# Row sums of squared differences: the first load pair recorded with the others instead of ahead of SyncE's drain

## The chip, the core and the metric

The kernel runs on one core of a Trainium2 chip. The time is device microseconds of one execution, here the median of three. Beside it stands a profile of one execution, taken by the hardware profiler. The engines of the core are TensorE (PE), VectorE (DVE), ScalarE (ACT), GpSimd (POOL) and SyncE (SP). SyncE computes nothing; its queue issues every DMA of this kernel. TensorE has no work in it.

## The reference

Two arrays of 1024 x 4096 float32 are subtracted, squared and summed along each row:

```python
def reference(x, y, axis):          # axis = -1
    return np.sum((x - y) ** 2, axis=axis).astype(np.float32)
```

So 33.55 MB are read from HBM and 4 KB are written.

## The kernel before

**Tiling.** Each of the 128 partitions takes 8 neighbouring rows (`R = B // P`, line 61), so a partition's share of `x` is one stretch of 8 x 4096 numbers in HBM. The tensors `X` and `Y` in SBUF hold 6 rows a partition (`H`, line 69). Rows 6 and 7 are loaded into the places of rows 0 and 1 once these are done with; column numbers are taken modulo 6 rows (lines 93 and 111).

**Loads.** `load_pair` (line 98) issues one DMA for a stretch of columns of `x` and one for the same stretch of `y`, both on SyncE, with a semaphore of their own. The first pair brings rows 0 to 3 (16,384 numbers a partition, 8.4 MB each for `x` and `y`), the second rows 4 and 5. Row 6 comes in two chunks (`w6`, line 75) and row 7 in six (`w7`, line 76). These eight pairs are issued behind a wait for ScalarE's second square (line 156), since they write over rows 0 and 1.

**Work on a row or chunk.** VectorE waits for the pair's landing, subtracts `Y` from `X` in place (`sub`, line 113), and then ScalarE squares and sums (line 121), or, for three of the chunks (`squares`, line 77), VectorE does so itself (line 129). `add_up` (line 144) adds the sums of chunks. The last chunk's square starts from the sum of the others, which stands in `head`. Then SyncE stores the 8 results of each partition (line 189) and waits for the store to land.

**What sets the order.** The kernel uses no scheduler; it records its instructions and puts them into the program's entry block itself, with the class `Program`. This block is made by the launch code (line 208 in the profile) and holds, engine by engine, a first part in which GpSimd sets four constants and all engines meet: each engine drains and raises a semaphore, GpSimd waits for all of them, raises a second semaphore, and each engine passes on that one. After this meeting the block ends in a branch for each engine. `Program._take` (line 24) takes what has been recorded since the last time; `_put` (line 29) inserts it at a given place in the entry block. There are two callers:

- `early` (line 32) inserts ahead of the drain of one engine, so what it moves runs on that engine ahead of the meeting;
- `close` (line 42), called once at the end, inserts all the rest ahead of the first branch, behind the meeting.

In the kernel before, `early` is called once, with SyncE, when only the first load pair has been recorded (lines 105 to 107):

```python
    load_pair(0, 4 * D)
    prog.early(mybir.EngineType.SP)
    load_pair(4 * D, 6 * D)
```

So SyncE issues the pair of rows 0 to 3 as its first instructions, then drains and meets the other engines, and then issues the pair of rows 4 and 5. All other work of the kernel stands behind the meeting on each engine. The two places and the two helpers that the diff does not touch but that decide where instructions land are in the code below.

Of the kernel before, what the change touches and what calls it, by code (L numbers as in the profile page):

```python
# [1 line left out]
_os.environ.setdefault("NEURON_RT_ULTRASERVER_MODE", "4")  # L2

# [3 lines left out]


class Program:

    def __init__(self, nc, tc):
        self.nc, self.hook = nc, tc.instruction_hook
        self.here = nc.cur_bb.bb.instructions
        self.entry = nc.main_func.blocks[0].instructions
        nc.remove_inst_callback(self.hook)  # L20
        self.lower, nc._always_lower_symbolic_ap = nc._always_lower_symbolic_ap, False
        self.before = len(self.here)

    def _take(self):
        taken = self.here[self.before :]
        del self.here[self.before :]
        return taken

    def _put(self, where):
        self.entry[where:where] = self._take()  # L30

    def early(self, engine):

        self._put(
            next(
                n
                for n, i in enumerate(self.entry)
                if i.engine == engine and str(i.opcode) == "Drain"
            )
        )  # L40

    def close(self):

        self._put(
            next(
                n for n, i in enumerate(self.entry) if str(i.opcode) == "UnconditionalBranch"
            )
        )
        self.nc._always_lower_symbolic_ap = self.lower
        self.nc.push_inst_callback(self.hook)  # L50


def kernel(tc, x, y, axis, out):
    nc = tc.nc
    P = nc.NUM_PARTITIONS
    F32 = mybir.dt.float32
    Square = mybir.ActivationFunctionType.Square
    mult, add = mybir.AluOpType.mult, mybir.AluOpType.add

    B, D = x.shape  # L60
    R = B // P


    xv = x.rearrange("(p r) d -> p (r d)", p=P)
    yv = y.rearrange("(p r) d -> p (r d)", p=P)
    ov = out.rearrange("(p r) -> p r", p=P)


    H = 6
    X = nc.alloc_sbuf_tensor("X", [P, H * D], F32).ap()  # L70
    Y = nc.alloc_sbuf_tensor("Y", [P, H * D], F32).ap()
    results = nc.alloc_sbuf_tensor("results", [P, R], F32).ap()
    junk = nc.alloc_psum_tensor("junk", [P, D], F32).ap()

    w6 = [3328, 768]
    w7 = [1280, 1024, 640, 512, 320, 320]
    squares = "ADAAAADD"
    assert sum(w6) == sum(w7) == D
    K = len(w7)
    part6 = nc.alloc_sbuf_tensor("part6", [P, len(w6)], F32).ap()  # L80
    part7 = nc.alloc_sbuf_tensor("part7", [P, K - 1], F32).ap()
    head = nc.alloc_sbuf_tensor("head", [P, 1], F32).ap()

    diffs = tc.alloc_semaphore("diffs")
    acts = tc.alloc_semaphore("acts")
    sums = tc.alloc_semaphore("sums")
    stored = tc.alloc_semaphore("stored")
    n = dict(diffs=0, acts=0, sums=0)

    prog = Program(nc, tc)  # L90

    def load(sem, src, dst, c0, c1):
        h0 = c0 % (H * D)
        nc.sync.dma_start(out=dst[:, h0 : h0 + c1 - c0], in_=src[:, c0:c1]).then_inc(sem, 16)  # L94

    loaded = []

    def load_pair(c0, c1):
        sem = tc.alloc_semaphore("loaded%d" % len(loaded))
        load(sem, xv, X, c0, c1)  # L100
        load(sem, yv, Y, c0, c1)
        loaded.append(sem)


    load_pair(0, 4 * D)
    prog.early(mybir.EngineType.SP)
    load_pair(4 * D, 6 * D)


    def sub(c0, w):  # L110
        h0 = c0 % (H * D)
        a = X[:, h0 : h0 + w]
        nc.vector.tensor_sub(out=a, in0=a, in1=Y[:, h0 : h0 + w]).then_inc(diffs, 1)  # L113
        n["diffs"] += 1

    def square_on_act(c0, w, acc):
        h0 = c0 % (H * D)
        nc.scalar.wait_ge(diffs, n["diffs"])
        if n["acts"]:
            nc.scalar.wait_ge(acts, n["acts"])  # L120
        nc.scalar.activation(  # L121
            out=junk[:, 0:w], in_=X[:, h0 : h0 + w], func=Square, accum_out=acc
        ).then_inc(acts, 1)
        n["acts"] += 1

    def square_on_dve(c0, w, acc, start):
        h0 = c0 % (H * D)
        nc.vector.wait_ge(diffs, n["diffs"])
        nc.vector.tensor_tensor_reduce(  # L129
            out=Y[:, h0 : h0 + w],  # L130
            in0=X[:, h0 : h0 + w],
            in1=X[:, h0 : h0 + w],
            scale=1.0,
            scalar=start,
            op0=mult,
            op1=add,
            accum_out=acc,
        ).then_inc(sums, 1)
        n["sums"] += 1

    def add_up(acc, parts, after=None):
        nc.vector.wait_ge(acts, n["acts"] if after is None else after)
        nc.vector.wait_ge(sums, n["sums"])  # L143
        nc.vector.tensor_reduce(  # L144
            out=acc, in_=parts, axis=mybir.AxisListType.X, op=add
        ).then_inc(sums, 1)
        n["sums"] += 1

    for r in range(6):
        if r in (0, 4):  # L150
            nc.vector.wait_ge(loaded[r // 4], 32)
        sub(r * D, D)
        square_on_act(r * D, D, results[:, r : r + 1])
        if r == 1:

            nc.sync.wait_ge(acts, 2)
            c0 = 6 * D
            for w in w6 + w7:
                load_pair(c0, c0 + w)
                c0 += w  # L160

    c0 = 6 * D
    for k, w in enumerate(w6 + w7):
        k7 = k - len(w6)
        if k7 == K - 1:
            add_up(head, part7)
        nc.vector.wait_ge(loaded[2 + k], 32)
        if k7 == K - 1:
            nc.vector.wait_ge(sums, n["sums"])  # L169
        sub(c0, w)  # L170
        if k7 < 0:
            acc = part6[:, k : k + 1]
        elif k7 < K - 1:
            acc = part7[:, k7 : k7 + 1]
        if k7 == K - 1:
            square_on_dve(c0, w, results[:, 7:8], head)
        elif squares[k] == "A":
            square_on_act(c0, w, acc)
        else:
            square_on_dve(c0, w, acc, 0.0)  # L180
        if k7 == 2:
            add_up(results[:, 6:7], part6, after=acts6)
        if k7 == -1:
            acts6 = n["acts"]
        c0 += w

    nc.sync.wait_ge(sums, n["sums"])
    nc.sync.wait_ge(acts, n["acts"])
    nc.sync.dma_start(out=ov, in_=results).then_inc(stored, 16)
    nc.sync.wait_ge(stored, 16)  # L190
    prog.close()


# [1 line left out]
_INS = ['x', 'y', 'axis']  # L195
_OUTS = [((1024,), 'float32')]

_NUMBERS = {'axis': -1}


# [26 lines left out]
```

## Time and profile before

| what | value |
|---|---|
| time, median of 3 runs | 86.94 us (86.9, 86.94, 87.03) |
| time of the profiled execution | 87.03 us |
| span of the profiled execution, first to last instruction | 85.2 us |
| bytes loaded, mean rate over the span | 33.56 MB, 394 GB/s |
| VectorE busy | 38.0 us (45%) |
| ScalarE busy | 30.7 us (36%) |
| first issue of a load to its landing (`x`, rows 0 to 3) | 21.9 us |
| issue of its `y` half to its landing | 40.8 us |
| first subtraction starts | 41.24 us |
| last sum ends, store issued | 82.88 us, 82.91 us |

Times in the profile count from the first instruction of the span. In lists of instructions the engine's name with a q (SPq, POOLq) stands for its sequencer: waits, drains and DMA issues, in which the engine itself is not busy. `L94` is line 94 of the kernel; all loads have that line, since `load` issues them. `L208` is the launch code with its meeting, `L222` the end of the program, where the engines meet again. `X<-in_x_dram` is a DMA or instruction that writes `X` from the array named. In the chain of waits each step is followed back to what released it; the shares there are of the span. A DMA share of 1.00 means that all 16 DMA engines of the core moved data all the time.

### The profile page before, as it was taken

How to read it: one execution, taken by the hardware profiler on the slowest of the kernel's cores; microseconds unless marked ns; L12 is line 12 of the kernel's file. 1: busy time of each engine (PE TensorE's matmuls, PEld its weight loads, DVE VectorE, ACT ScalarE, POOL GpSimd, SP SyncE). 2: the span in 40 equal slices, each digit the busy share in tenths (PEclk: the TensorE clock that was granted, in tenths of full speed). 3: DMA queues.
4: the chain of work that ended last, by engine and by line, in shares of the span. 5: the costliest groups of instructions: out<-in, count | busy, mean ns of one | idle time of the engine just before them, and what ended most of it. 6: DMA issues, size and time to landing. Idle time of an engine off the chain costs nothing.

```text
span 85.2 us, 122 instructions
## 1 busy us (share of the span) xinstructions
DVE 38.0 (45%) x22; ACT 30.7 (36%) x23; POOL 0.2 (0%) x4
## 2 busy tenths in 40 slices
DVE  0000000000000000000699999995599999997670
ACT  4100000000000000000005979797924979999800
POOL 0000000000000000000000000000000000000000
DMA  9559999997499999993899979997999999999700
GB/s 492 246 246 492 492 492 492 492 492 338 215 431 492 492 492 492 492 461 154 369 492 477 415 338 492 492 400 338 412 412 437 372 426 423 408 401 383 262 0 2
DMA packets 3024, 33.56 MB, mean 394 GB/s; under 512 B 464, under 2 KB 976, under 8 KB 2256
## 3 DMA queue, kind: packets, MB, share of 16 engines
q1 hardware_dynamic: 3024, 33.56, 93.8%
HBM read 33.55 MB, written 0.00 MB: 394 GB/s over the span
## 4 chain that ended last, share of the span: by engine, by line
DMA 63%; SPq 15%; DVE 13%; ACT 4%; issue 1%; DVEq 0%
DMA Y<-in_y_dram 63%; SPq L94 15%; DVE X L113 11%; ACT junk L121 4%; DVE Y L129 1%; DVE head L144 0%; DVEq L169 0%; DVEq L143 0%; DVE part L129 0%; DVEq L222 0%
## 5 line engine op out<-in xcount | busy, mean ns | idle before, releaser
L113 DVE TENSOR_TENSOR X<-X,Y 128x4096 f32<-128x4096 f32 (+7 forms) x14 | 35.8, 2594 | 44.7 <-DMA Y<-in_y_dram 44.6
L121 ACT ACTIVATE junk<-X 128x4096 f32<-128x4096 f32 (+5 forms) x11 | 28.1, 2550 | 49.0 <-DVE X L113 48.6
L121 ACT ACTIVATION_READ_ACCUMULATOR junk<-X 128x1 f32 x11 | 2.0, 186 | 0.0
L121 ACT ACT_TABLE_LOAD x1 | 1.3, 1283 | 1.3 <-PEq L208 1.3
L129 DVE CUSTOM_DVE_ANT_0 Y<-X 128x768 f32<-128x768 f32 (+1 forms) x2 | 1.4, 724 | 0.1
L129 DVE CUSTOM_DVE_ANT_0 Y<-X,head 128x320 f32<-128x320 f32 x1 | 0.6, 552 | 0.0
L144 DVE TENSOR_REDUCE head<-part 128x1 f32<-128x5 f32 x1 | 0.2, 158 | 0.1
L129 DVE DVE_READ_ACCUMULATOR2_ANT part<- 128x1 f32 x2 | 0.2, 82 | 0.0
L144 DVE TENSOR_REDUCE results<-part 128x1 f32<-128x2 f32 x1 | 0.1, 150 | 0.0
L208 POOL MEMSET const-bfloat16-1.0<- 128x1 bf16 x1 | 0.1, 101 | 0.0
L208 POOL MEMSET const-uint8-127<- 128x1 uint8 x1 | 0.1, 101 | 0.0
L208 POOL MEMSET const-float32-0.0<- 128x1 f32 x1 | 0.1, 98 | 0.2 <-issue 0.2
L208 POOL MEMSET const-float32-1.0<- 128x1 f32 x1 | 0.1, 98 | 0.0
L129 DVE DVE_READ_ACCUMULATOR2_ANT results<- 128x1 f32 x1 | 0.1, 83 | 0.0
## 6 DMA issues: line engine op xcount, KB each, us to landing
X<-in_x_dram SPq DMA_DIRECT2D x1, 4096.0 KB, 49.7
Y<-in_y_dram SPq DMA_DIRECT2D x1, 4096.0 KB, 59.0
X<-in_x_dram SPq DMA_DIRECT2D x1, 1664.0 KB, 10.9
Y<-in_y_dram SPq DMA_DIRECT2D x1, 1664.0 KB, 14.6
X<-in_x_dram SPq DMA_DIRECT2D x1, 640.0 KB, 16.7
Y<-in_y_dram SPq DMA_DIRECT2D x1, 640.0 KB, 17.8
X<-in_x_dram SPq DMA_DIRECT2D x1, 512.0 KB, 18.6
Y<-in_y_dram SPq DMA_DIRECT2D x1, 512.0 KB, 19.4
```

The costliest lines, as they stand in the source:

```text
L94: nc.sync.dma_start(out=dst[:, h0 : h0 + c1 - c0], in_=src[:, c0:c1]).then_inc(sem, 16)
L113: nc.vector.tensor_sub(out=a, in0=a, in1=Y[:, h0 : h0 + w]).then_inc(diffs, 1)
L121: nc.scalar.activation(out=junk[:, 0:w], in_=X[:, h0 : h0 + w], func=Square, accum_out=acc).then_inc(acts, 1)
L129: nc.vector.tensor_tensor_reduce(out=Y[:, h0 : h0 + w], in0=X[:, h0 : h0 + w], in1=X[:, h0 : h0 + w], scale=1.0, scalar=start, op0=mult, o ...
L144: nc.vector.tensor_reduce(out=acc, in_=parts, axis=mybir.AxisListType.X, op=add).then_inc(sums, 1)
L208: nc = _bacc.Bacc("TRN2", target_bir_lowering=False, num_devices=1)
```

## The change

The call of `early` is deleted. The first pair is then taken by `close` with all the rest, and stands behind the meeting of the entry block, ahead of the second pair. `early` itself stays, and nothing calls it. The whole diff:

```diff
     load_pair(0, 4 * D)
-    prog.early(mybir.EngineType.SP)
     load_pair(4 * D, 6 * D)
```

The order of each engine's instructions is otherwise the same; on SyncE the changed program has the drain and the wait of the meeting first, then the X and Y loads of rows 0 to 3, then those of rows 4 and 5, then the wait for ScalarE and the chunks of rows 6 and 7. All line numbers behind 106 are lower by one.

## The prediction, made before the result was known

> **What bounds the kernel now.** I read the chain of waits first, to see which work ended last, then the DMA slices and windows, to see whether that work has slack anywhere, then the opening of the timeline and the group of instructions of line 208, because that is where the change acts.
>
> The head of the chain of work that ended last, from the page:
>
> ```profile
> ## 4 chain that ended last, share of the span: by engine, by line
> DMA 63%; SPq 15%; DVE 13%; ACT 4%; issue 1%; DVEq 0%
> ```
>
> The same chain in order of time, cut to its roots and its end (start us, us, what):
>
> ```profile
> 0.43 40.79 DMA Y<-in_y_dram
> ...
> 50.04 3.72 ACT junk L121 x2
> ...
> 67.14 13.24 DMA Y<-in_y_dram
> 80.38 0.02 issue
> 80.40 0.51 DVE X L113
> ```
>
> The chain starts at the very first load pair: the Y half of rows 0 to 3 is issued at 0.43 us and lands 40.79 us later. Everything after hangs on it, because VectorE's first subtraction waits for that landing, ScalarE's second square (done at 53.76) lets SyncE issue rows 6 and 7, and the last transfer of the chain ends at 80.38. From there to the last sum at 82.9 VectorE works almost without a break.
>
> Does the load stream ever pause, so that a late start could be made up? The DMA view and a table of windows (us, then busy time of the engines, clock, DMA share, GB/s):
>
> ```profile
> q1 hardware_dynamic: 3024, 33.56, 93.8%
> ...
> 0.00:20.00 20.00, 0.00 (x0) 1.28 (x1) 0.20 (x4) 1.00 1.00 419
> 20.00:40.00 20.00, 0.00 (x0) 0.00 (x0) 0.00 (x0) 1.00 0.97 419
> 40.00:60.00 20.00, 17.43 (x4) 12.42 (x7) 0.00 (x0) 1.00 0.99 426
> 60.00:80.00 20.00, 18.18 (x11) 16.25 (x14) 0.00 (x0) 1.00 1.01 406
> ```
>
> The share of the 16 DMA engines that is busy is 0.97 to 1.01 in all four quarters (a packet is booked in the window where it starts, hence values over 1). The trace's packet records say the same more sharply: between the first load packet at 1.00 us and the stream's tail near 80 us there is no moment without packets in flight, and 16 of them are in flight on average. So the kernel is one unbroken transfer of 33.55 MB, with a start of about 1.0 us ahead of it and a tail of VectorE and the store behind it.
>
> The start, from the timeline (start us, us, instruction):
>
> ```profile
> 0.00 0.38 SPq L94 DMA_DIRECT2D X<-in_x_dram  x1
> ...
> 0.33 0.10 POOL L208 MEMSET const-uint8-127<- 128x1 uint8 x1
> 0.43 0.42 SPq L94 DMA_DIRECT2D Y<-in_y_dram  x1
> 1.25 1.28 ACT L121 ACT_TABLE_LOAD   x1 [1.25 <-PEq L208]
> 1.26 0.33 SPq L94 DMA_DIRECT2D X<-in_x_dram  x1
> ```
>
> SyncE issues the first pair as its first two instructions. Line 208, the launch code, then has all engines meet: each drains, tells GpSimd through a semaphore, and GpSimd releases them. SyncE's second pair stands behind that release, at 1.26. The group of line 208 (duration in ns, then first and last start):
>
> ```profile
> L208 POOLq DRAIN  x1: 179/179/179, 0.3 to 0.3; - x1
> ...
> L208 SPq DRAIN  x1: 125/125/125, 0.9 to 0.9; - x1
> L208 SPq EVENT_SEMAPHORE  x1: 17/17/17, 1.2 to 1.2; - x1
> ```
>
> **The change, part by part.** It deletes the one call that puts what has been recorded so far ahead of SyncE's drain. The built order of the changed kernel shows the result: the first pair now stands where the second stood, directly behind the release of the meeting, and the second pair follows it. No instruction is added or removed on any engine, and only SyncE's order differs.
>
> *What it removes.* Two issues (0.38 and 0.42 us, with a gap of 0.05) ahead of SyncE's drain. In the trace's own records the drain runs from 0.905 to 1.030 us. All other engines have arrived earlier: VectorE and ScalarE drain at 0.12 and 0.13, TensorE at 0.31, GpSimd ends its drain at 0.479, behind its four memsets. So SyncE is the last one at the meeting today, and it holds the meeting by 1.030 - 0.479 = 0.55 us.
>
> *What the release costs.* From SyncE's drain end at 1.030 GpSimd sees all arrivals at 1.056, sends the release at 1.134, SyncE passes at 1.176, and the next issue starts at 1.259: 0.229 us in all.
>
> *The new start.* SyncE drains at once. The last arrival is then GpSimd at 0.479, whose instructions I take to stay where they are. Adding 0.229 gives 0.708. One link differs, since GpSimd now waits for its own arrival and not for SyncE's: at the meeting at the kernel's end, where GpSimd too is late, its drain ends at 85.022 and it sees the arrivals at 85.066, 0.044 after, in place of 0.026. That gives 0.726. I take 0.72. The X issue moves from 0.00 to 0.72, and the Y issue behind it from 0.43 to about 1.15.
>
> *Bounds.* From below: if GpSimd were in time as well and only the release remained, the issue would stand at 0.007 (a drain with nothing ahead of it, as SyncE's drains at the end have) + 0.229 = 0.24. From above: if the release did not move at all, because something other than SyncE's arrival sets it, the issue would stand at today's 1.26. The value lies at 0.72 by the nearest row, GpSimd's drain.
>
> The Trainium skill, page "Runtime: NRT & Kernel Launch", section "The ~15µs preamble/postamble breakdown", puts a crossing of the five engines on the runtime's own sync barrier at some 355 ns, at 44 ns a hop. By that figure the start would be 0.479 + 0.355 + 0.083 (from passing to issue) = 0.92, an estimate, and the time 87.86; the row of this trace has 0.15 for that crossing, and the sum goes by the row.
>
> *What it moves.* The first load packet starts 1.00 us after the X issue today; the same distance gives 1.72. As the stream has no pause, its end moves by the same 0.72, and with it every landing. No later step is late on its own account: the second pair's issue moves from 1.26 to about 1.6, but its packets come up only after 16.8 MB of the first pair, near 41 us, so this is covered by 39 us. The issues of rows 6 and 7 start at 53.77, behind ScalarE's second square, which moves with the Y landing; the queue ahead of them still holds the second pair until 60.67, so they keep 6.9 us of cover. SyncE's long issues (up to 3.44 us, behind a full queue) move along with the queue. VectorE waits for landings up to 80.40 (idle 0.20, 0.43, 0.47 and 0.23 us ahead of its last four subtractions that waited, each ended by a Y transfer), so it cannot swallow a late landing.
>
> *What gets earlier.* The release comes 0.55 us earlier for the other engines. ScalarE's table load moves from 1.25 to about 0.7, but ScalarE has nothing to do until 45.70, and VectorE until the first landing. This gain is worth nothing.
>
> The Trainium skill's page "DMA: Bandwidth & Descriptors", section "Issuing engines are not separate DMA queues", calls the sequencer's time to start a DMA usually small beside the DMA itself. Read as a rule about this change it speaks for no difference (86.94): 0.38 us of issuing against 21.9 us of transfer. The issue is not lengthened here, though, it starts later, and a stream without a pause cannot hide a late start.
>
> **Sum.** The profiled execution took 87.03 us, with a span of 85.2, so 1.8 us lie around the span, which I leave as they are. 87.03 + 0.72 = 87.75 for that execution; it is the slowest of the three shown, 0.09 over their median. On the median: 86.94 + 0.72 = **87.66 us**. One small unknown goes the other way: should the time count from the first instruction, and SyncE's drain start no earlier than the other engines' (0.12) where its first issue stood at 0.00, then 0.12 is not counted and it is 87.54.
>
> **Rivals.**
> 1. *The release does not move.* The table of waits puts SyncE's wait at the meeting down to TensorE (line 208), as it does ScalarE's table load; if TensorE's sequencer set the release, it would stay at 1.17 and the first issue would come at 1.26: 86.94 + 1.26 = 88.20. Against it: TensorE's drain is recorded at 0.31, and GpSimd's reaction comes 26 ns after the end of SyncE's drain.
> 2. *The start-up excess pays it back* (not slower). The first sixteen 64 KB packets take 3.14 us in the mean, the next sixteen 2.42. If these 0.72 us come from the launch's own traffic (32-byte packets of the launch are recorded up to 0.08 us before the first issue) and not from the first reads themselves, starting 0.72 later finds the path free, and all of the delay is recovered: 86.94. It decides once more than 0.55 of the 0.72 come back. For it: the launch's packets come close before. Against it: they end about 1.1 us ahead of the first load packet, so they are gone before it anyway.
> 3. *The move is hidden.* If the tail were set by VectorE's own work from some early point, the landings would have room and the time would stay at 86.94. The idle times before VectorE's last waiting subtractions, all ended by transfers, speak against it.
>
> **How the numbers follow.** A measurement of this kernel can tell about 0.2% (0.17 us) from no change. Forecast (0.5 to 0.9 us more): 0.84. Rival 1: 0.08. Rival 2: 0.04. Rival 3: 0.02. An unnamed gain by a changed order of the first packets: 0.02. So slower 0.92, same 0.06, faster 0.02. The range takes both bounds of the start, 86.94 + 0.24 = 87.18 and 86.94 + 1.26 = 88.20, rounded; rivals 2 and 3 stay outside it. The forecast's own range is 87.45 to 87.85.
>
> **What would show it.** In the changed profile SyncE's first issue stands at 0.6 to 0.8 us from the start of the span, behind an event of line 208; GpSimd's two events of that line stand near 0.52 and 0.60 in place of 1.06 and 1.13; the first subtraction starts near 41.96 in place of 41.24, the second square frees SyncE near 54.5, and the last sum ends near 83.6; the DMA slices stay full; the distance from the X issue to its landing stays 21.9 us. Wrong would be: a first issue at 1.2 or later (rival 1), first packets near 2.4 us (rival 2), or a first subtraction 0.7 later with the end where it was (rival 3).

## The result, and the profile after

| | before | after |
|---|---|---|
| median of 4 runs, us | 86.98 (86.90 to 87.06) | 87.67 (87.53 to 87.68) |
| profiled execution, us | 87.03 | 87.68 |
| its span, us | 85.2 | 85.9 |

The ratio is 1.0075, with a 95% interval of 1.0058 to 1.0093: slower by 0.69 us, or 0.5 to 0.8 us by the interval. The whole interval lies above the 0.2% that the prediction took as the least that can be told from no change, so this is a loss. The predicted time, 87.66, is 0.01 off. That it is so near is in part luck: the kernel before has a median of 86.98 here and had 86.94 when the sum was made, and by the newer figure the same sum gives 87.70.

The opening of the timeline of the changed kernel (start us, us, instruction):

```profile
...
0.33 0.10 POOL L207 MEMSET const-uint8-127<- 128x1 uint8 x1
0.72 1.28 ACT L120 ACT_TABLE_LOAD   x1 [0.72 <-PEq L207]
0.73 0.38 SPq L94 DMA_DIRECT2D X<-in_x_dram  x1
1.16 0.43 SPq L94 DMA_DIRECT2D Y<-in_y_dram  x1
1.63 0.42 SPq L94 DMA_DIRECT2D X<-in_x_dram  x1
```

The first load is issued at 0.73 us, where it stood at 0.00. ScalarE's table load comes earlier by 0.53; past_drain, below, shows that nothing follows from that.

The group of line 207, the meeting, in the changed kernel (duration in ns, then first and last start):

```profile
L207 POOLq EVENT_SEMAPHORE  x2: 17/17/17, 0.5 to 0.6; - x2
L207 SPq DRAIN  x1: 7/7/7, 0.0 to 0.0; - x1
...
L207 POOLq DRAIN  x1: 179/179/179, 0.3 to 0.3; - x1
...
L207 SPq EVENT_SEMAPHORE  x1: 17/17/17, 0.6 to 0.6; - x1
```

SyncE's drain is now the first instruction of the span and takes 7 ns in place of 125. GpSimd's two events of the meeting stand at 0.5 and 0.6 in place of both at 1.1. To the nanosecond, from the trace's own records: GpSimd's drain ends at 0.482, it sees all arrivals at 0.526, releases at 0.605, and SyncE passes at 0.646.

The chain of waits of the changed kernel, in order of time, with cuts marked by dots:

```profile
...
1.16 40.86 DMA Y<-in_y_dram
42.01 0.02 issue
42.03 8.77 DVE X L112 x2
50.81 0.02 issue
50.83 3.72 ACT junk L120 x2
...
67.84 13.19 DMA Y<-in_y_dram
81.03 0.02 issue
81.06 0.50 DVE X L112
...
```

The chain has the same members with the same lengths (40.86 us for the first Y landing, before 40.79; 13.19 for the last of the chain, before 13.24; ScalarE 3.72 in both). It has only been shifted: the Y issue from 0.43 to 1.16, the end of the last transfer from 80.38 to 81.03. The windows of the changed kernel (us, busy time of the engines, clock, DMA share, GB/s) show the stream as full as before:

```profile
0.00:20.00 20.00, 0.00 (x0) 1.28 (x1) 0.20 (x4) 1.00 1.00 419
20.00:40.00 20.00, 0.00 (x0) 0.00 (x0) 0.00 (x0) 1.00 0.97 419
40.00:60.00 20.00, 17.43 (x4) 11.63 (x7) 0.00 (x0) 1.00 0.97 419
60.00:80.00 20.00, 17.64 (x10) 16.29 (x13) 0.00 (x0) 1.00 0.99 400
```

### The profile page after: what moved, and what is told of

Its sections match the earlier page's. It is cut to its first block, busy times and chain, and to the rows that moved or that the text cites. A ratio compares the mean times of both kernels' runs of the same rounds, so it can differ in the third digit from the quotient of the medians.

```text
span 85.9 us, 122 instructions
## 1 busy us (share of the span) xinstructions
DVE 38.0 (44%) x22; ACT 30.7 (36%) x23; POOL 0.2 (0%) x4
## 4 chain that ended last, share of the span: by engine, by line
DMA 63%; SPq 15%; DVE 13%; ACT 4%; issue 1%; DVEq 0%
DMA Y<-in_y_dram 63%; SPq L94 15%; DVE X L112 11%; ACT junk L120 4%; DVE Y L128 1%; DVE head L143 0%; DVEq L168 0%; DVEq L142 0%; DVE part L128 0%; DVEq L221 0%
```

## The experiments

The theory to be tested: the kernel is one unbroken stream of loads, and its time follows the issue of the stream's first bytes, one for one; where the other instructions of the entry block stand costs nothing. Against it stood that something else in the reordered start costs the time: the table load that now meets the first packets, the meeting itself, the number of issues behind it, or a cold path whose penalty moves about. Seven kernels were run, each timed against the kernel before on the same chip. "Stream" below is from the start of the first to the end of the last load packet of the profiled execution, from the trace's packet records. The ratios are to the runs of the kernel before that were made beside each kernel, with medians of 86.92 and 86.93 us; single ones of them lie between 86.70 and 87.53, and the 86.98 in the table is from the runs beside the changed kernel.

| kernel | X issue, us | first packet, us | stream, us | median, us | ratio to before, 95% interval |
|---|---|---|---|---|---|
| before | 0.00 | 1.00 | 79.73 | 86.98 | |
| after | 0.73 | 1.73 | 79.67 | 87.67 | 1.0075, 1.0058 to 1.0093 |
| past_drain | 0.08 | 1.07 | 79.42 | 86.90 | 1.0007, 0.9994 to 1.0020 |
| x_only | 0.00 | 1.00 | 79.57 | 86.94 | 1.0002, 0.9985 to 1.0019 |
| late_pool_after | 2.47 | 3.49 | 79.48 | 89.34 | 1.0289, 1.0272 to 1.0305 |
| late_pool_before | 0.00 | 1.00 | 79.77 | 86.84 | 0.9989, 0.9976 to 1.0002 |
| row_first | 0.00 | 0.99 | 79.55 | 86.83 | 0.9988, 0.9970 to 1.0006 |
| both_pairs | 0.00 | 1.00 | 79.53 | 86.86 | 0.9999, 0.9985 to 1.0013 |

The seventh, sliver_first, has two starts of the stream and is told below.

### Behind the drain, ahead of the wait (past_drain)

```diff
-    prog.early(mybir.EngineType.SP)
+    prog.early(mybir.EngineType.SP, 1)
     load_pair(4 * D, 6 * D)
```

The added argument moves the place of insertion one instruction on, past SyncE's drain.

> The first pair stands between SyncE's drain and its wait for the release: SyncE arrives at the meeting at once, as in the changed kernel, but issues at once too. Theory (only the start of the load stream counts): the X issue stands at 0.05 to 0.1 us, the time is that of the kernel before plus as much, 87.0 to 87.1 us, ratio 1.000 to 1.002. Rival (the changed kernel is slower because the first packets now meet ScalarE's table load, which moved to 0.72 us): the table load stands at 0.72 here too, so part of the 0.7 us stays, 87.3 us or more.

The timeline of this kernel:

```profile
0.08 0.36 SPq L95 DMA_DIRECT2D X<-in_x_dram  x1
...
0.49 0.42 SPq L95 DMA_DIRECT2D Y<-in_y_dram  x1
0.73 1.28 ACT L122 ACT_TABLE_LOAD   x1 [0.73 <-PEq L209]
```

The table load stands where it stands in the changed kernel, and the time is that of the kernel before: 86.90 us, ratio 1.0007. So neither the earlier meeting nor the table load beside the first packets costs anything that can be measured here. The median is below the 87.0 to 87.1 that was expected: the 0.08 us of delay is within the interval and can't be told from nothing.

### Only the X half early (x_only)

```diff
-    load_pair(0, 4 * D)
-    prog.early(mybir.EngineType.SP)
+    first = tc.alloc_semaphore("loaded0")
+    load(first, xv, X, 0, 4 * D)
+    prog.early(mybir.EngineType.SP)
+    load(first, yv, Y, 0, 4 * D)
+    loaded.append(first)
     load_pair(4 * D, 6 * D)
```

> Only the X half of the first pair stands ahead of SyncE's drain, its Y half behind the meeting. Theory (the start of the stream counts, the Y half has some 20 us of X ahead of it): the time of the kernel before, 86.98 us, ratio 0.999 to 1.001; the Y issue stands at about 0.8 to 0.95 us, its landing does not move. Rival (every issue moved behind the meeting costs its share): half of the 0.7 us, 87.3 us, ratio 1.004.

From its chain of waits:

```profile
0.77 40.41 DMA Y<-in_y_dram
41.18 0.02 issue
```

The Y half is issued at 0.77 us in place of 0.43 and lands at 41.18, in the kernel before at 41.22. The time stays, 86.94 us and a ratio of 1.0002. The first transfer in the chain of waits is that of Y, and yet its issue could be 0.34 us later for nothing: the X half ahead of it in the queue keeps the DMA engines busy until it lands at 21.8 us.

### A later meeting, behind the loads or ahead of them (late_pool_after, late_pool_before)

Both kernels put one more memset ahead of GpSimd's drain, on a tensor that nothing else uses; one is the changed kernel with it, the other the kernel before.

```diff
+    slack = nc.alloc_sbuf_tensor("slack", [P, 2048], F32).ap()
...
+    nc.gpsimd.memset(slack, 0.0)
+    prog.early(mybir.EngineType.Pool)
     load_pair(0, 4 * D)
```

> The changed kernel with one more GpSimd memset of 128x2048 float32 ahead of GpSimd's drain. Theory (GpSimd is the last at the meeting and every microsecond of the release is one of the time): with d the memset's duration as its row shows it (I expect 1.5 to 5 us), the X issue moves by d less what overlaps, and the time is 87.67 + d, within 0.15 us. First packets again some 0.7 us longer than the later ones. Rival (start-up traffic of the launch or a fixed cost of the order of issues makes the 0.7): the time grows by less than d, by up to 0.7 us less, and the first packets take 2.4 us.

> The kernel before with the same memset of 128x2048 float32 ahead of GpSimd's drain. Theory: the meeting comes late by d, but the stream has started ahead of it, so the time stays at 86.98, ratio 0.999 to 1.001; the second pair's issue and ScalarE's table load move by about d and nobody waits for them. Rival (a later meeting costs by itself): 86.98 + d.

The timelines, first that of the changed kernel with the memset, then that of the kernel before with it:

```profile
0.37 1.80 POOL L106 MEMSET slack<- 128x2048 f32 x1
2.46 1.28 ACT L123 ACT_TABLE_LOAD   x1 [2.46 <-PEq L210]
2.47 0.37 SPq L95 DMA_DIRECT2D X<-in_x_dram  x1
```

```profile
0.00 0.38 SPq L95 DMA_DIRECT2D X<-in_x_dram  x1
...
0.37 1.80 POOL L106 MEMSET slack<- 128x2048 f32 x1
0.43 0.42 SPq L95 DMA_DIRECT2D Y<-in_y_dram  x1
2.47 1.28 ACT L124 ACT_TABLE_LOAD   x1 [2.47 <-PEq L211]
2.47 0.33 SPq L95 DMA_DIRECT2D X<-in_x_dram  x1
```

The memset takes 1.80 us and the release moves by 1.74 us, so GpSimd is the engine that sets the meeting once SyncE no longer does, and in the second of these kernels too, where SyncE's drain ends at 1.03. Where the first pair stands behind the meeting, the time goes to 89.34, 1.67 over the changed kernel; over the kernel before the ratio of 1.0289 makes 2.51 us (2.36 to 2.65) and the medians of the runs made together differ by 2.41, beside an X issue that is 2.47 us late. Where the pair stands ahead, the same late meeting, table load and second pair cost nothing: 0.9989, with an interval that holds 1. The time expected for the first was 87.67 + 1.80 = 89.47 within 0.15, and it came 0.13 below.

These two runs also answer the rival on the first packets: with the issue at 2.47 the first sixteen still take 2.95 us in the mean, beside 2.42 for the next sixteen. In the other kernels of the table whose first packets are of 64 KB (all but row_first) they take 3.04 to 3.14. So most of the excess comes with the start of the stream, whenever that is; a later start took 0.1 to 0.2 us off it at most.

### How much must stand early (sliver_first, row_first)

```diff
-    load_pair(0, 4 * D)
-    prog.early(mybir.EngineType.SP)
+    first = tc.alloc_semaphore("loaded0")
+    load(first, xv, X, 0, 128)
+    prog.early(mybir.EngineType.SP)
+    load(first, xv, X, 128, 4 * D)
+    load(first, yv, Y, 0, 4 * D)
+    loaded.append(first)
     load_pair(4 * D, 6 * D)
```

This is sliver_first; row_first has `D` (4096) in place of 128. The first wait of VectorE asks for three transfers, 48 in place of 32.

> Only 128 of the 16,384 columns of X (64 KB) stand ahead of SyncE's drain, the rest of the first pair behind the meeting. Theory (the bulk of the stream must start early; the 0.7 us by which the first packets are longer come with each start of the stream): the sliver covers 0.15 us at 433 GB/s, then the queue runs dry until about 1.75 us; the first 65 KB packets behind it again take about 3.1 us; time 87.5 to 87.7, ratio 1.006 to 1.009. Rival (the first packets are long because engines and queue are cold, and anything early warms them): the 65 KB packets take 2.4 us and the time is 86.9 to 87.1.

> Only row 0 of X (2 MB, 4.8 us of the stream) stands ahead of SyncE's drain, the rest of the first pair behind the meeting. Theory (enough early bytes to bridge the meeting are all that counts): the next X issue stands at about 0.75 us, its first packets would be ready near 1.75, and the queue still holds row 0 until about 5.9 us, so the time is that of the kernel before, 86.9 to 87.0, ratio 0.999 to 1.001, or up to 0.3 us less if the first packets of 16 KB start the stream with less loss than those of 64 KB. Rival (the whole pair has to stand early): 87.3 or more.

The issue of the rest of X in the chain of waits of sliver_first, followed by that of Y:

```profile
0.78 0.33 SPq L94
1.11 0.05 issue
1.16 40.67 DMA Y<-in_y_dram
```

Sliver_first took 87.62 us, ratio 1.0083 (1.0060 to 1.0106), like the changed kernel: the sliver lands at 1.96 us, but the first packet of the bulk, whose issue stands at 0.78, starts at 1.74, as in the changed kernel (1.73), and its first sixteen packets take 3.07 us beside 2.40 for the next. From there to the end of the stream it is 79.49 us, as in the others. The expectation had the queue dry from 0.15 us behind the sliver's start. The packet records show something else: the sliver's 128 packets of 512 B are strung out from 1.00 to 1.62 us, so that only 0.11 us ahead of the bulk have no packet at all. But at some 26 ns a packet they make 0.21 us of work for each of the 16 DMA engines, so these were idle most of that time all the same. An early trickle of this size gains nothing that can be measured, and warms nothing.

Row_first is at 0.9988: the 2 MB of row 0 keep the engines busy until the rest, issued at 0.77, follows; its packet records have no gap. Its first sixteen packets, of 16 KB, take 1.24 us beside 0.63, an excess of 0.61 where the 64 KB ones have 0.5 to 0.7, so smaller packets start the stream no cheaper to speak of, and the gain of up to 0.3 us that was left open didn't come.

### Both pairs early (both_pairs)

```diff
     load_pair(0, 4 * D)
-    prog.early(mybir.EngineType.SP)
     load_pair(4 * D, 6 * D)
+    prog.early(mybir.EngineType.SP)
```

> Both pairs of rows 0 to 5 stand ahead of SyncE's drain, so SyncE holds the meeting until about 1.9 us. Theory: nobody waits for the meeting but ScalarE's table load, which has until 45 us; the time stays that of the kernel before, ratio 0.999 to 1.001, and the X issue at 0.00. Rival (holding the meeting costs by itself): 86.94 plus about 0.8 us, ratio 1.009.

SyncE now holds the meeting: its drain ends at 2.07 us and ScalarE's table load comes at 2.29. The time stays: 0.9999.

None of these kernels beats the kernel before by more than its interval. Among the forms that were tried, all that issue the X half, or even one row of it, ahead of SyncE's wait at the meeting are equally good.

## Why the prediction was right

*The new start.* The working put the X issue at 0.72, from GpSimd's drain end, the crossing and the step from passing to issue; it stands at 0.73, well inside the two bounds. The release did move, so TensorE's name in the table of waits was indeed only that of an engine long done (the same view names TensorE's sequencer for the table load in late_pool_after, where GpSimd's memset plainly sets the time). That GpSimd comes next was argued from one row; late_pool_after shows it.

The Trainium skill's figure of some 355 ns for the crossing ("Runtime: NRT & Kernel Launch", "The ~15µs preamble/postamble breakdown") would have put the time at 87.86. Here it took 0.646 - 0.482 = 0.164 us; the measurement decides. That figure is for the runtime's own barrier, which is not in this trace.

*One for one.* The term was 0.72 and the medians differ by 0.69. Within the two profiled executions the shift isn't quite constant: 0.73 at the X issue, 0.79 at the first subtraction, 0.65 at the end of the last transfer of the chain. The table's streams suggest why: the same bytes took 79.4 to 79.8 us from one profiled execution to the next, with no visible relation to the start, and the stream of the changed kernel is the shorter by 0.06. Single runs of the kernel before scatter by more than that, from 86.74 to 87.38 in one set of 29. So the difference between 0.65 and 0.73 is no sign of a hidden gain; with one profiled execution of each kernel, that it is scatter is argued and not shown.

*What was costed at nothing.* The earlier release for ScalarE and VectorE brought nothing (past_drain, whose release is as early, is no faster), and the later second pair cost nothing (late_pool_before has it at 2.47). The caution that the time might count from a later first instruction was not needed: SyncE's drain is the first instruction of the span, as its first issue was, and the time around the span is 1.78 us in both.

*The rivals.* A release that does not move would have shown the first issue at 1.26; it is at 0.73. The start-up excess paid nothing back that counts: the first sixteen packets take 3.08 us in the changed kernel beside 3.14 before, and still 2.95 with the late memset. A hidden move is excluded by the result and by the chain, whose end moved with its start.

*A rule weighed.* The Trainium skill's remark that starting a DMA is usually small beside the DMA ("DMA: Bandwidth & Descriptors", "Issuing engines are not separate DMA queues") holds for the issue here, 0.38 us against 22 us from issue to landing. It doesn't say that the start's place is free, and x_only and late_pool_after show the two sides of it: the Y issue, behind 8.4 MB of X, could be 0.34 us late for nothing, the first issue could not.

## What to carry to other kernels

In a kernel that one unbroken stream of loads bounds, look at the first load's issue and ask what stands ahead of it: here each microsecond there was one of the time (0.73 us cost 0.69, and 2.47 us cost 2.4 to 2.5), and the launch code's meeting of the engines is among the things that can stand there. What has to be ahead of that meeting is only enough bytes to keep the DMA engines busy until the next issue's packets are ready: 2 MB were enough, more brought nothing, and 64 KB brought nothing either. Sizes between these were not tried. A step that is moved is priced from the last arrival at the meeting, which changes when the one that held it leaves: here from SyncE to GpSimd.

## What the runs showed of the hardware that was not expected

Each start of the stream loses time once, whenever it comes: the first sixteen 64 KB packets take 0.5 to 0.7 us longer than those that follow (2.95 to 3.14 us against 2.42), whether they start at 1.0 or at 3.5 us, and behind a sliver of 64 KB as well. What sets this excess was not tried.

From the start of the first issue to the first packet 0.99 to 1.02 us pass in all kernels with one start. From the end of that issue it is 0.62 us in the changed kernel, 0.63 in the kernel before and in past_drain, and at most 0.65 (late_pool_after). In sliver_first the bulk's issue takes 0.33 us instead of 0.38; its first packet comes 0.95 us from the start of it and 0.62 from its end. The Trainium skill gives about 0.6 us for the first byte of such a DMA ("DMA: Bandwidth & Descriptors", "Latency and other measured facts"); these traces agree if one counts from the end of the issuing instruction, not from its start, to the start of the first packet.

In past_drain SyncE issues loads between its drain and its wait for the release; ScalarE, VectorE and TensorE are released at 0.65 to 0.66 us, and SyncE itself passes at 0.97, when its issues are done. So SyncE could do work of its own inside the meeting without holding the others.
